# Where the weight sums stand among the blocks of an up-projection: from behind the even steps to behind the odd ones, and other side work the other way round

## The chip, the cores and the metric

The kernel runs on one core of a Trainium2 chip. A core has a matrix engine (TensorE, PE in the profile, with its weight loads as PEld), a vector engine (VectorE, DVE), a scalar engine (ScalarE, ACT), a general one (GpSimd, POOL) and a synchronising one (SyncE, SP). Each works through its own queue in order, and they wait for each other by semaphores. DMA transfers are issued from such queues too: here SP issues weight loads and residuals, POOL issues the transfers of the sums that this case is about. The metric is the device time of one execution in microseconds (us).

## The reference

The program computes two layers of an encoder on 512 tokens with 1024 channels. A layer has four branches (a convolution module and three kinds of attention), gates, an output projection, and then the part that matters here, a feed-forward network with a convolution of width 3 along the tokens:

```python
def _conv_ffn(h, w_up, conv_w, conv_b, w_down):
    u = _depthwise_conv(h @ w_up, conv_w, conv_b)
    gate, up = jnp.split(u, 2, axis=-1)
    return (jax.nn.silu(gate) * up) @ w_down

def reference(x, ...):
    for l in range(DEPTH):                    # DEPTH = 2
        h = _rmsnorm(x, g_mix[l])
        ...                                   # branches, gates
        x = x + mixed @ w_out[l]
        x = x + _conv_ffn(_rmsnorm(x, g_ffn[l]), w_up[l], ffn_conv_w[l], ffn_conv_b[l], w_down[l])
    return x
```

D_FF is 2816, so w_up is 1024 x 5632 and w_down 2816 x 1024. Everything is float32.

## The kernel before

All products run as pairs of rounded values: each operand is split into a high part and the rest (w_hi and w_lo for weights, xh and xl for activations), and each product is three matmuls, hi*hi, hi*lo, lo*hi (lines 243 to 245 of `prod`). The weights come as units of 128 x 1024 by SP (w_raw, L218); ACT writes w_hi (L222), DVE writes w_lo (L224).

**Up-projection** (`ffn`). 22 steps i; each has two blocks, the gate's (s = 0) and the up half's (s = 1), of 24 matmuls each into one of four PSUM banks (`mm`). Behind a block, DVE reads the bank with U = mm * RB (L892), which frees it, and ACT and DVE do the convolution (cy, L895 to L897), the gate (L901) and the product fl (L908). RB is the row of 1/rms of the tokens, broadcast to all partitions: `finish_norm` writes rstd to DRAM (row, L330), reads it back broadcast (raw, L334), both on POOL's queue, and ACT copies it (RB, L338). Since the matmuls run on the unnormalised input, RB is first needed by the U of the first block.

**Down-projection** (`down`). It is a Strassen-like scheme over pairs of the hidden blocks: 11 pairs j, each with a "quad" of w_down (four blocks of 128 x 512: b11, b12, b21, b22) and sums and differences of its blocks and of the activations. The activations' part, `split_pair`, is done for the first six pairs during the up-projection (`EARLY` names the steps) and for the others in `down`. The weights' part is `weight_sums(l, j)`, during the up-projection: four DVE operations (L955 to L958: t3, b12, t2, b21) on the quad in SBUF, four POOL transfers of 256 KB to DRAM (L961), and then `load_quad(l, j + 1)`, two POOL transfers of 512 KB (L948). The two buffers of a quad (`w_more`) are used again by the next quad, and in `down` by the raw weights of each third and fourth unit. So quad j+1 is loaded only when sums j are written.

`down` works through 22 units of 12 matmuls for the first two groups of products and then further units for the other three. Its first six matmuls write the mm banks (A) that the blocks of step 20 used, the next six the banks (B) of step 21's blocks, so each bank's first matmul has to wait for the U that reads it.

`turn_res(d)`, in layer 1 only, loads a tile of the residual, transposes it on DVE (L920) and writes it to DRAM in four transfers on SP (L923), since the last layer's output is token by token.

**What sets the order.** The code is written with a tile framework; a scheduler places each engine's instructions by priority, which follows the order of the code, and by when they can run in its own model. `issue_after` and `after_mm` tie the weight sums to the last matmul before them (`last_mm`), so they can't be placed ahead of it. `split_pair` and `turn_res` have no such tie. In this kernel `weight_sums(l, i // 2)` stands behind the two blocks of each even step i (0, 2, ..., 20), before the U's of that step.

## Time and profile before

| quantity | value |
|---|---|
| median of 3 runs | 1561.07 us (1560.98 to 1561.43) |
| the profiled execution, its own time | 1563.17 us |
| its span in the profile | 1561.4 us |
| PE busy | 1552.9 us, 99% of the span |
| PE clock granted | 1.00 |
| DVE busy | 1220.4 us, 78% |
| ACT busy | 833.7 us, 53% |
| POOL busy | 176.9 us, 11% |
| up-projection of layer 0, blocks | about 436 to 674 us |
| up-projection of layer 1, blocks | about 1212 to 1452 us |

Start times in the rows count from the start of the span. A row of the timeline has the start, the duration, the engine, the line, the operation, what it writes and reads, and in brackets how long its engine had been idle before it and what ended that. "SPq" and "POOL ... DMA" rows are the issue of a transfer; when the transfer lands is told by the DMA views.

### The profile page before, as it was taken

How to read it: one execution, taken by the hardware profiler on the slowest of the kernel's cores; microseconds unless marked ns; L12 is line 12 of the kernel's file. 1: busy time of each engine (PE TensorE's matmuls, PEld its weight loads, DVE VectorE, ACT ScalarE, POOL GpSimd, SP SyncE). 2: the span in 40 equal slices, each digit the busy share in tenths (PEclk: the TensorE clock that was granted, in tenths of full speed). 3: DMA queues.
4: the chain of work that ended last, by engine and by line, in shares of the span. 5: the costliest groups of instructions: out<-in, count | busy, mean ns of one | idle time of the engine just before them, and what ended most of it. 6: DMA issues, size and time to landing. Idle time of an engine off the chain costs nothing.

```text
span 1561.4 us, 20467 instructions
## 1 busy us (share of the span) xinstructions
PE 1552.9 (99%) x7198; PEld 1292.2 (83%) x7198; DVE 1220.4 (78%) x2083; ACT 833.7 (53%) x1419; POOL 176.9 (11%) x308
## 2 busy tenths in 40 slices
PE   9999999999999999999999999999999999999999
PEld 8888888888888888888888888888888788888887
DVE  6689988765679997796676899887655699987964
ACT  5678767333444443364458687772434444443643
POOL 0102002122011111100001020012120111111000
PEclk9999999999999999999999999999999999999999
DMA  7622222232646655576556422223226676665675
GB/s 231 196 93 82 84 83 82 95 100 93 213 162 209 193 190 186 200 235 212 185 183 182 120 68 86 81 72 105 95 94 222 170 228 217 213 218 194 222 226 167
DMA packets 103607, 245.41 MB, mean 157 GB/s; under 512 B 27600, under 2 KB 29520, under 8 KB 103504
## 3 DMA queue, kind: packets, MB, share of 16 engines
q1 hardware_dynamic: 89392, 196.37, 39.9%
q0 software_dynamic: 13824, 47.20, 8.9%
q8 instruction: 57, 0.93, 0.3%
q10 hardware_dynamic: 288, 0.52, 0.1%
q14 instruction: 46, 0.38, 0.1%
HBM read 203.15 MB, written 35.66 MB: 153 GB/s over the span
## 4 chain that ended last, share of the span: by engine, by line
PE 91%; DVE 4%; ACT 3%; issue 1%; DMA 1%; POOL 0%; SPq 0%; ACTq 0%; DVEq 0%; POOLq 0%
PE mm L243 21%; PE mm L244 21%; PE mm L245 21%; PE aux L1023 2%; PE aux L1024 2%; PE aux L1025 2%; PE mm L439 2%; PE mm L440 2%; PE mm L441 2%; PE mm L1024 2%; PE mm L1025 2%; PE mm L1023 2%; PE aux L709 2%; DVE w_lo L224 1%; PE aux L440 1%; PE aux L441 1%
## 5 line engine op out<-in xcount | busy, mean ns | idle before, releaser
L222 ACT ACTIVATE w_hi<-w_raw 128x1024 fp32r<-128x1024 f32 (+1 forms) x305 | 318.5, 1044 | 355.0 <-PE mm L244 193.7
L243 PE MATMUL mm<-xh,w_hi 128*128 128x512 f32 x1280 | 499.9, 391 | 1.8 <-DVE U L892 1.8
L245 PE MATMUL mm<-xh,w_lo 128*128 128x512 f32 x1280 | 498.7, 390 | 0.0
L244 PE MATMUL mm<-xl,w_hi 128*128 128x512 f32 x1280 | 498.6, 390 | 0.0
L224 DVE TENSOR_TENSOR w_lo<-w_raw,w_hi 128x1024 fp32r<-128x1024 f32 (+1 forms) x305 | 369.1, 1211 | 88.2 <-ACT w_hi L222 86.0
L243 PEld LDWEIGHTS mm<-xh,w_hi 128*128 128x128 f32 x1280 | 240.3, 188 | 51.3 <-DVE U L892 2.2
L245 PEld LDWEIGHTS mm<-xh,w_lo 128*128 128x128 f32 x1280 | 240.3, 188 | 50.4
L244 PEld LDWEIGHTS mm<-xl,w_hi 128*128 128x128 f32 x1280 | 240.4, 188 | 48.8
L813 POOL TENSOR_TENSOR mx<-mx,t 128x512 f32<-128x512 f32 x44 | 66.9, 1529 | 428.6 <-DVE t L812 327.4
L377 DVE SCALAR_TENSOR_TENSOR cv<-cv,prm 128x512 f32<-128x512 f32 x120 | 93.8, 781 | 0.7
L892 DVE TENSOR_TENSOR U<-mm,RB 128x512 f32<-128x512 f32 x88 | 60.2, 687 | 41.5 <-PE mm L245 31.3
L895 ACT ACTIVATE cy<-U,prm 128x512 f32<-128x512 f32 x88 | 70.7, 807 | 38.5 <-DVE U L892 38.4
L783 DVE TENSOR_TENSOR t<-mm,RB 128x512 f32<-128x512 f32 x64 | 44.0, 688 | 47.8 <-PE mm L245 47.4
L439 PE MATMUL mm<-w_hi,xh 128*128 128x512 f32 x192 | 76.4, 398 | 0.4 <-DVE V L567 0.4
L440 PE MATMUL mm<-w_lo,xh 128*128 128x512 f32 x192 | 75.0, 390 | 0.0
L441 PE MATMUL mm<-w_hi,xl 128*128 128x512 f32 x192 | 74.8, 390 | 0.0
L696 ACT ACTIVATE e<-e,rl 128x256 f32<-128x256 f32 (+2 forms) x96 | 57.4, 598 | 23.4 <-DVE rl L695 23.1
L897 DVE SCALAR_TENSOR_TENSOR cy<-U,prm,cy 128x512 f32<-128x512 f32 x88 | 65.7, 748 | 1.6
L901 ACT ACTIVATE fth<-cy 128x512 f32<-128x512 f32 x44 | 27.9, 633 | 71.4 <-DVE cy L897 71.3
L896 DVE SCALAR_TENSOR_TENSOR cy<-U,prm,cy 128x512 f32<-128x512 f32 x88 | 65.5, 746 | 0.4 <-ACT cy L895 0.4
L689 ACT ACTIVATE e<-e,nm 128x256 f32<-128x256 f32 (+2 forms) x96 | 57.6, 600 | 2.7
L717 DVE TENSOR_TENSOR pt<-aux,pt 128x256 fp32r<-128x256 f32 (+2 forms) x96 | 50.9, 530 | 2.4 <-ACT pt L716 1.2
(292 smaller groups left out, 2592.5 us busy)
## 6 DMA issues: line engine op xcount, KB each, us to landing
w_raw<-W SPq DMA_DIRECT2D x223, 512.0 KB, 3.6
quad<-W POOLq DMA_DIRECT2D x44, 512.0 KB, 5.2
w_raw<-W SPq DMA_DIRECT2D x66, 256.0 KB, 3.7
sums<-t POOLq DMA_DIRECT2D x44, 256.0 KB, 3.3
sums<-quad POOLq DMA_DIRECT2D x44, 256.0 KB, 3.9
w_raw<-sums SPq DMA_DIRECT2D x44, 256.0 KB, 3.9
w_raw<-sums SPq DMA_DIRECT2D x22, 512.0 KB, 4.7
res<-xn SPq DMA_DIRECT2D x24, 256.0 KB, 2.0
```

What stands on the lines that cost most here:

```text
L222: w = nc.scalar.activation(hi[:, s], raw[:, s], AF.Copy)
L224: nc.vector.tensor_tensor(lo[:, s], raw[:, s], hi[:, s].bitcast(F32), ALU.subtract)
L243: mm(ps, lhsT=wh, rhs=xh, start=start, stop=False)
L244: mm(ps, lhsT=wh, rhs=xl, start=False, stop=False)
L245: self.last_mm = mm(ps, lhsT=wl, rhs=xh, start=False, stop=stop)
L377: self.after_mm(v.scalar_tensor_tensor(acc, u[:, t:t + S], w(t), acc, ALU.mult, ALU.add))
L439: mm(pss[b], lhsT=self.Xh[k][:, t], rhs=hi[:, s], start=k == 0, stop=False)
L440: mm(pss[b], lhsT=self.Xh[k][:, t], rhs=lo[:, s], start=False, stop=False)
L441: self.last_mm = mm(pss[b], lhsT=self.Xl[k][:, t], rhs=hi[:, s], start=False, stop=k == KT - 1)
L813: (v if n == ORDER[3] and d >= 6 else nc.gpsimd).tensor_tensor(m, m, t, ALU.add)
L895: nc.scalar.activation(y, u[:, 1:513], AF.Identity, scale=w(1), bias=self.par('ffn_conv_b', c))
L897: v.scalar_tensor_tensor(y, u[:, 2:514], w(2), y, ALU.mult, ALU.add)
```

## The change

Three tables or rules move. The weight sums of pair j go behind the blocks of the odd step 2j + 1 instead of the even step 2j, but for the last pair, j = 10, which stays behind step 20. `EARLY` moves four of its six steps by one or two. `turn_res(d)` goes from the odd step 2d + 1 to the even step 2d + 2. No work is added or taken away.

```diff
-EARLY = (3, 6, 10, 13, 17, 20)
+EARLY = (4, 6, 10, 12, 16, 18)
+
+SUMS = (1, 3, 5, 7, 9, 11, 13, 15, 17, 19, 20)
 ...
-            if i % 2 == 0:
+            if i in SUMS:
 
                 with self.tc.issue_after(self.last_mm.ins):
-                    self.weight_sums(l, i // 2)
+                    self.weight_sums(l, SUMS.index(i))
 ...
-            if last and i % 2 == 1 and i // 2 < KT:
-                self.turn_res(i // 2)
+            if last and i % 2 == 0 and 0 < i // 2 <= KT:
+                self.turn_res(i // 2 - 1)
```

Below the tables every line number of the changed kernel is two higher. PE's own order is the same in both kernels. Three places show how the other engines' order moves.

**POOL, at the start of layer 1's up-projection.** row and raw are the two transfers of the broadcast, quad the load of the first quad, sums the writes of the first weight sums. Before:

```order
L948 DMA quad<-W 128x1024 x2
L330 DMA row<-rstd 128x4
L961 DMA sums_11901<-t_11895 128x512
L334 DMA raw<-row 128x512
L961 DMA sums_11901<-quad 128x512
L961 DMA sums_11901<-t_11896 128x512
```

and after the change:

```order
L950 DMA quad<-W 128x1024 x2
L332 DMA row<-rstd 128x4
L336 DMA raw<-row 128x512
L963 DMA sums_11977<-t_11971 128x512
L963 DMA sums_11977<-quad 128x512
```

The first sums' write stood between row and raw, and now stands behind both. (In layer 0 raw stood directly behind row already.)

**DVE, the last two sums of layer 0's up-projection.** U0 to U3 are the reads of the banks of successive blocks, t3 the first operation of a pair's sums. Before:

```order
L892 TENSOR_TENSOR U3_4497<-mm_6256,RB_4559 128x512
L224 TENSOR_TENSOR w_lo_6335<-w_raw_6333,w_hi_6334 128x1024
L896 SCALAR_TENSOR_TENSOR cy1_6295<-U3_4497,prm_73,cy1_6295 128x512
L897 SCALAR_TENSOR_TENSOR cy1_6295<-U3_4497,prm_73,cy1_6295 128x512
L908 TENSOR_TENSOR fl19_6299<-cy1_6295,fth_6292 128x512
L892 TENSOR_TENSOR U0_4488<-mm_6301,RB_4559 128x512
L224 TENSOR_TENSOR w_lo_6410<-w_raw_6408,w_hi_6409 128x1024
L896 SCALAR_TENSOR_TENSOR cy0_6375<-U0_4488,prm_73,cy0_6375 128x512
L897 SCALAR_TENSOR_TENSOR cy0_6375<-U0_4488,prm_73,cy0_6375 128x512
L955 TENSOR_TENSOR t3_6363<-quad_6208,quad_6207 128x512
L892 TENSOR_TENSOR U1_4491<-mm_6332,RB_4559 128x512
L224 TENSOR_TENSOR w_lo_6441<-w_raw_6439,w_hi_6440 128x1024
```

and after the change, from the end of pair 9's sums to the start of pair 10's:

```order
L958 TENSOR_TENSOR quad_6116<-quad_6116 128x512
L898 SCALAR_TENSOR_TENSOR cy1_6314<-U3_4497,prm_73,cy1_6314 128x512
L959 TENSOR_TENSOR t2_6292<-quad_6117,quad_6116 128x512
L899 SCALAR_TENSOR_TENSOR cy1_6314<-U3_4497,prm_73,cy1_6314 128x512
L960 TENSOR_TENSOR quad_6117<-quad_6117,t2_6292 128x512
L910 TENSOR_TENSOR fl19_6318<-cy1_6314,fth_6311 128x512
L894 TENSOR_TENSOR U0_4488<-mm_6320,RB_4559 128x512
L226 TENSOR_TENSOR w_lo_6410<-w_raw_6408,w_hi_6409 128x1024
L898 SCALAR_TENSOR_TENSOR cy0_6394<-U0_4488,prm_73,cy0_6394 128x512
L899 SCALAR_TENSOR_TENSOR cy0_6394<-U0_4488,prm_73,cy0_6394 128x512
L894 TENSOR_TENSOR U1_4491<-mm_6351,RB_4559 128x512
L957 TENSOR_TENSOR t3_6382<-quad_6303,quad_6302 128x512
```

Pair 10's first operation stands behind the U1 that it stood ahead of, and pair 9's sums, which stood four blocks ahead of pair 10's, now stand two ahead. Pair 9's first operation stands directly behind the two cy of block 38 and ahead of U3.

**DVE, from the last sums to the last U of layer 0.** Before:

```order
L958 TENSOR_TENSOR quad_6208<-quad_6208,t2_6364 128x512
L908 TENSOR_TENSOR fl20_6386<-cy1_6382,fth_6379 128x512
L892 TENSOR_TENSOR U2_4494<-mm_6407,RB_4559 128x512
L224 TENSOR_TENSOR w_lo_6526<-w_raw_6524,w_hi_6525 128x1024
L896 SCALAR_TENSOR_TENSOR cy0_6471<-U2_4494,prm_73,cy0_6471 128x512
L1002 TENSOR_TENSOR pfl11_6506<-fl13_5758,pxl0_6504 128x512
L897 SCALAR_TENSOR_TENSOR cy0_6471<-U2_4494,prm_73,cy0_6471 128x512
L1004 TENSOR_TENSOR sum_6511<-fl12_5682,fl13_5758 128x256
L1005 TENSOR_TENSOR fl12_5682<-fl12_5682 128x256
L1006 TENSOR_TENSOR sum_6511<-sum_6511,fl12_5682 128x256
L1010 TENSOR_TENSOR fl13_5758<-fl13_5758,sum_6511 128x256
L892 TENSOR_TENSOR U3_4497<-mm_6438,RB_4559 128x512
```

and after the change:

```order
L960 TENSOR_TENSOR quad_6303<-quad_6303,t2_6383 128x512
L910 TENSOR_TENSOR fl20_6405<-cy1_6401,fth_6398 128x512
L894 TENSOR_TENSOR U2_4494<-mm_6407,RB_4559 128x512
L226 TENSOR_TENSOR w_lo_6526<-w_raw_6524,w_hi_6525 128x1024
L1004 TENSOR_TENSOR pfl11_6506<-fl13_5777,pxl0_6504 128x512
L898 SCALAR_TENSOR_TENSOR cy0_6471<-U2_4494,prm_73,cy0_6471 128x512
L899 SCALAR_TENSOR_TENSOR cy0_6471<-U2_4494,prm_73,cy0_6471 128x512
L1006 TENSOR_TENSOR sum_6511<-fl12_5667,fl13_5777 128x256
L1007 TENSOR_TENSOR fl12_5667<-fl12_5667 128x256
L1008 TENSOR_TENSOR sum_6511<-sum_6511,fl12_5667 128x256
L894 TENSOR_TENSOR U3_4497<-mm_6438,RB_4559 128x512
L226 TENSOR_TENSOR w_lo_6544<-w_raw_6542,w_hi_6543 128x1024
```

The sequence is nearly the same: pfl11 moves ahead of both cy, and L1010 (now L1012) from ahead of the last U to behind it.

## The prediction

> **What bounds the kernel now.** I read the page from the top: the span and the busy shares, then the chain that ended last, then the groups with the idle time before them.

> ```profile
> span 1561.4 us, 20467 instructions
> PE 1552.9 (99%) x7198; PEld 1292.2 (83%) x7198; DVE 1220.4 (78%) x2083; ACT 833.7 (53%) x1419; POOL 176.9 (11%) x308
> PE 91%; DVE 4%; ACT 3%; issue 1%; DMA 1%; POOL 0%; SPq 0%; ACTq 0%; DVEq 0%; POOLq 0%
> L243 PE MATMUL mm<-xh,w_hi 128*128 128x512 f32 x1280 | 499.9, 391 | 1.8 <-DVE U L892 1.8
> ```

> PE (the matmuls) is busy in all but 1561.4 - 1552.9 = 8.5 us, and the chain runs over it for 91% of the span. The change adds and removes no matmul, so it can win no more than the PE gaps near what it moves, and it loses whatever new gap it opens. So the second view is the table of stretches over the two up-projections (columns: stretch, us, busy time of PE, PEld, DVE, ACT, POOL with counts, PE clock, DMA share, GB/s).

> ```profile
> 436.00:674.00 238.00, 238.00 (x1056) 197.23 (x1055) 203.89 (x303) 106.76 (x139) 35.71 (x66) 1.00 0.58 191
> 1212.00:1452.00 240.00, 238.20 (x1056) 197.06 (x1055) 207.39 (x311) 106.03 (x139) 35.75 (x66) 1.00 0.67 210
> ```

> Layer 0's up-projection has no PE gap, layer 1's has 240.00 - 238.20 = 1.80 us. That is all there is to win in the stages that the change touches: 2 us. DVE, with 203.89 of 238 us, is 86% busy there; it is the engine on which a misplaced wait would hurt.

> **Where the 1.80 us come from.** The timeline of layer 1's start, POOL's queue and what hangs on it, and then the same steps of layer 0:

> ```profile
> 1221.27 0.55 POOL L330 DMA_DIRECT2D row<-rstd  x1 [47.19 <-DVE rstd L275]
> 1221.92 0.55 POOL L961 DMA_DIRECT2D sums<-t  x1
> 1226.47 0.54 POOL L334 DMA_DIRECT2D raw<-row  x1 [4.00 <-DMA row<-rstd]
> 1232.75 0.39 PE L245 MATMUL mm<-xh,w_lo 128*128 128x512 f32 x1
> 1233.05 1.11 ACT L338 ACTIVATE RB<-raw 128x512 f32<-128x512 f32 x1 [9.87 <-DMA raw<-row]
> 1234.19 1.89 DVE L892 TENSOR_TENSOR U<-mm,RB 128x512 f32<-128x512 f32 x3 [8.42 <-ACT RB L338]
> 1234.94 0.50 PE L243 MATMUL mm<-xh,w_hi 128*128 128x512 f32 x1 [1.80 <-DVE U L892]
> ```
> ```profile
> 444.15 0.55 POOL L330 DMA_DIRECT2D row<-rstd  x1 [46.27 <-DVE rstd L275]
> 446.55 0.54 POOL L334 DMA_DIRECT2D raw<-row  x1 [1.85 <-DMA row<-rstd]
> 450.20 1.12 ACT L338 ACTIVATE RB<-raw 128x512 f32<-128x512 f32 x1 [3.23 <-DMA raw<-row]
> ```

> The four mm banks fill, and the fifth block cannot start until U (L892) has read the first, for which it needs RB, the broadcast of the row of rstd. In layer 0 the two POOL transfers stand next to each other: 446.55 - 444.15 = 2.40 us to the second, 450.20 - 446.55 = 3.65 more to RB. In layer 1 a 256 KB transfer of the first weight sums stands between them, and the same steps take 1226.47 - 1221.27 = 5.20 and 1233.05 - 1226.47 = 6.58. PE's matmuls start 0.23 apart, so PE was ready at 1232.75 + 0.23 = 1232.98 and started at 1234.94: 1.96 us lost, and 0.11 more in the first matmul (0.50 for 0.39), 2.07 together.

> **Part 1: the first sums leave the first step.** After the change POOL's queue in layer 1 reads row, raw, then sums, as in layer 0. By layer 0's distances RB would start at 1221.27 + 2.40 + 3.65 = 1227.32. It needs to start by 1232.98 - (1234.94 - 1233.05) = 1231.09, so 3.8 us are to spare. Bounds: the whole 2.07 is won, or nothing, where the row is late for another reason. I take -2.0, since the nearer row is layer 0's. In layer 0 nothing waits there, so nothing is won.

> What could hold the row otherwise: SP had just issued two writes of transposed residual.

> ```profile
> 1219.68 0.96 SPq L923 DMA_DIRECT2D resT<-xn  x2
> 1217.38 0.70 DVE L920 STREAM_TRANSPOSE xn<-xr 128x512 f32<-128x512 f32 x1
> 1245.07 0.69 DVE L908 TENSOR_TENSOR fl<-cy,fth 128x512 f32<-128x512 f32 x1
> 1245.80 0.42 DVE L1004 TENSOR_TENSOR sum<-fl,fl 128x256 f32<-128x256 f32 x1
> ```

> [...]

> **Part 2: EARLY and turn_res.** The last two rows show the first early pair's first instruction 0.73 us behind fl, in the second step, while the table says step 3: the scheduler takes this work when its inputs exist, not where the code stands. The same for the transposes, the first of which runs in the first block, three blocks ahead of its code. In the order of the changed kernel both stay there. Their cost is nothing, hidden in DVE's idle 32 us of these 240. If they did move, all eight transposes of 0.70 us are 5.6 us of DVE work, still inside that; each step has a share of 1.5 us.

> **Part 3: the spacing at the end.** The sums of pair j need quad j, whose load waits until the sums of pair j-1 have been written and freed its buffer. Of before, sums follow each other every two steps, 21.75 us (661.76 - 640.01 in the rows below). In the changed order they still do, but for the last: pair 9 goes behind step 19 and pair 10 behind step 20. On DVE pair 9 now starts behind the cy of 650.24, so at 650.9, and pair 10 behind the U of 663.70, so at 664.3. The gap is 13.4 us.

> ```profile
> 640.01 0.68 DVE L955 TENSOR_TENSOR t<-quad 128x512 f32<-128x512 f32 x1
> 650.40 0.54 POOL L948 DMA_DIRECT2D quad<-W  x1 [0.56 <-DMA sums<-quad]
> 1418.30 0.69 DVE L955 TENSOR_TENSOR t<-quad 128x512 f32<-128x512 f32 x1
> 1429.53 0.54 POOL L948 DMA_DIRECT2D quad<-W  x1 [1.59 <-DMA sums<-quad]
> quad<-W POOLq DMA_DIRECT2D x44, 512.0 KB, 5.2
> quad<-W POOLq DMA_DIRECT2D x2, 512.0 KB, 6.4
> DMA to landing us min/median/max: 2.6/4.8/7.1
> 650.24 0.75 DVE L897 SCALAR_TENSOR_TENSOR cy<-U,prm,cy 128x512 f32<-128x512 f32 x1
> 661.76 0.69 DVE L955 TENSOR_TENSOR t<-quad 128x512 f32<-128x512 f32 x1
> 663.70 0.69 DVE L892 TENSOR_TENSOR U<-mm,RB 128x512 f32<-128x512 f32 x1 [1.25 <-PE mm L245]
> ```

> From t of one pair to the issue of the second half of the next quad it takes 650.40 - 640.01 = 10.39 us in layer 0 and 1429.53 - 1418.30 = 11.23 in layer 1 (these are the last pairs but one, with the same neighbours on DVE). The fifth row is the page's median landing of a quad's half, 5.2; the sixth is the DMA view of 640 to 661 alone, 6.4; the seventh the shortest and longest of all transfers of that tile, 2.6 and 7.1. The turn-round is then 10.39 + 5.2 = 15.6 to 10.39 + 6.4 = 16.8 us, at the ends 13.0 to 18.3. So DVE, which takes its instructions in order, stands at t for 2.2 to 3.4 us, from nothing to 4.9 at the ends. I take 3.0, nearer to the two measured here (16.8, and 11.23 + 5.2 = 16.4).

> [...]

> What is queued behind t, and who waits:

> ```profile
> 664.61 1.23 DVE L224 TENSOR_TENSOR w_lo<-w_raw,w_hi 128x1024 fp32r<-128x1024 f32 x1 [0.22 <-ACT w_hi L222]
> 674.46 0.43 DVE L1010 TENSOR_TENSOR fl<-fl,sum 128x256 f32<-128x256 f32 x1
> 674.80 0.69 DVE L892 TENSOR_TENSOR U<-mm,RB 128x512 f32<-128x512 f32 x1
> 676.42 0.39 PE L1023 MATMUL mm<-w_hi,pe 128*128 128x512 f32 x1
> 677.36 1.22 DVE L224 TENSOR_TENSOR w_lo<-w_raw,w_hi 128x1024 fp32r<-128x1024 f32 x1 [1.27 <-ACT w_hi L222]
> 680.04 0.39 PE L1024 MATMUL mm<-w_lo,pfh 128*128 128x512 f32 x1
> 681.16 1.23 DVE L224 TENSOR_TENSOR w_lo<-w_raw,w_hi 128x1024 fp32r<-128x1024 f32 x1 [1.32 <-ACT w_hi L222]
> 696.69 0.50 PE L1024 MATMUL mm<-w_lo,pfh 128*128 128x512 f32 x1 [0.17 <-DVE w_lo L224]
> 1453.10 0.68 DVE L892 TENSOR_TENSOR U<-mm,RB 128x512 f32<-128x512 f32 x1
> 1454.71 0.39 PE L1023 MATMUL mm<-w_hi,pe 128*128 128x512 f32 x1
> ```

> From the w_lo at 664.61 DVE works without a pause: the splits of the weights of down's first two units, the rest of the sums, U of the blocks 42 and 43. Without L1010, which now stands behind U, that is 674.46 - 664.61 = 9.85 us, with t (0.6 from start to start) 10.45. Unstalled, the last U would start at 664.30 + 10.45 = 674.75, as before. Down's tenth matmul (676.42) writes the bank that this U reads; the distance from a U to its matmul was 1234.94 - 1234.19 = 0.75, so U must start by 675.67. The slack is 0.92: a stall of 3.0 delays PE by 2.1 us. In layer 1 the slack is 1454.71 - 0.75 - 1453.10 = 0.86: 2.1 again. With stalls of 2.2 to 3.5 it is 1.3 to 2.6 per layer.

> A second customer: the third and fourth weight units of down take their buffers from the quads, so their loads start when these sums are written. Their t is 5.5 us later than before (667.3 for 661.76), less the 2.2 that DVE idled between t and the w_lo at 664.61 (2.85 apart, 0.6 of it t): the sums leave about 3.3 us later. In layer 0 the third unit's w_lo ended 680.04 - 677.36 - 1.22 = 1.46 ahead of its matmul, the fourth's about 0.38 (681.16 + 1.23 = 682.39, and its matmul 2.72, twelve starts, behind 680.04). With PE itself 2.1 later the third just makes it, 1.46 + 2.1 - 3.3 = 0.3, and the fourth is short by 3.3 - 2.1 - 0.4 = 0.8. Bounds: 0, if its load meets fewer others when it starts later, and 1.0, the 0.8 and 0.2 for the wait at 696.69 (0.17), which grows from the same slack; I take 0.5, the middle. In layer 1 I add nothing: the wait for w_lo at 696.69 has no counterpart there.

> **Sum.** -2.0 (start of layer 1) + 2.1 + 0.5 (end of layer 0's up-projection) + 2.1 (layer 1's) = +2.7 us. The profiled execution took 1563.17, its span 1561.4, so 1.8 lie around it; the median of the runs is 1561.07, 2.1 lower, and the sum is put on it: 1561.07 + 2.7 = 1563.8 us.

> **The rivals.**

> A. *The quad comes in time.* For it: the shortest landing of 2.6 with 10.39 gives 13.0 < 13.4, and U has 0.9 of slack. Against it: the medians. Then only the gain is left: 1561.07 - 2.0 = 1559.1 us. Chance 0.13.

> B. *The row is not freed.* The two resT writes in the rows above, not the sums, held it. For it: they are on SP just ahead of row, in layer 1 alone. Against it: the sums' issue stands right between row and raw. Then 1561.07 + 2.1 + 2.1 + 0.5 = 1565.8. Chance 0.12.

> C. *Slower: the last quad comes later still.* The long issue time of layer 1 (11.23) and the long landing of layer 0 (6.4) meet, since the load now runs 11 us later, beside the first weights of down. It is on DVE at pair 10's t and decides from a stall of 3.5 on. For it: the two landings of 6.4. Against it: the median of 5.2 over 44 loads. The stall is 11.23 + 6.4 - 13.4 = 4.2, PE's delay 3.3 in each layer, the 0.5 as above: 1561.07 - 2.0 + 6.6 + 0.5 = 1566.2. Chance 0.15.

> D. *The change doesn't do what it says*: if the scheduler had put the sums back, the time would be 1561.1. The order of the changed kernel speaks against it. Chance 0.02.

> **The numbers.** My forecast has 0.55, and the rest of 0.03 is for a gap outside these stages that closes too. The forecast is 1563.8, its own range 1562.2 (stalls of 2.2, nothing at the fourth unit) to 1565.3 (stalls of 3.5 and the full 1.0). The range to hold the time 8 times in 10 takes in rival A, whose price is a landing inside the measured ones, and most of C: 1559.0 to 1566.5. A measurement of this kernel tells about 0.2%, 3.1 us, from no change, so 1564.2 is the bound to slower: of my own case some 0.36 lies below and 0.19 above it. Same: 0.36 + 0.13 + 0.02 = 0.51. Slower: 0.19 + 0.12 + 0.15 = 0.46. Faster: the rest, 0.03.

> **What the profile would show.** Right: in layer 1 raw's issue about 2.4 us behind row's and no PE idle behind U there; a DVE idle of 2 to 3.5 us in front of the last t, ended by the DMA quad<-W; a PE idle of 1.3 to 2.6 at the tenth matmul of down, ended by U, in both layers. Wrong: t of pair 10 without idle (A); raw again 4 us or more behind row (B); PE idle over 3 per layer (C); or pairs of sums not 13.4 us apart.

## The result

| | us |
|---|---|
| before, median of 4 runs | 1561.25 (1560.98 to 1562.31) |
| changed, median of 4 runs | 1569.70 (1569.10 to 1569.92) |
| ratio | 1.0052, 95% interval 1.0040 to 1.0064 |
| predicted | 1563.8, range 1559.0 to 1566.5 |

The change makes the kernel 8.4 us slower: a clear loss, and outside the range. The profiled execution of the changed kernel took 1569.92 us with a span of 1568.2, so like is compared with like when the two spans are: 1568.2 - 1561.4 = 6.8 us.

The page of the changed kernel has this in the rows that were shown of before:

```profile
span 1568.2 us, 20470 instructions
PE 1555.9 (99%) x7198; PEld 1292.8 (82%) x7198; DVE 1216.8 (78%) x2083; ACT 834.6 (53%) x1419; POOL 177.1 (11%) x308
quad<-W POOLq DMA_DIRECT2D x44, 512.0 KB, 5.4
```

PE is not only idle for longer (12.3 us for 8.5). It is also *busy* for 3.0 us longer with the same 7198 matmuls, for which the prediction had no term. The waits of PE and of DVE, in order of size, lead to both (the columns are the time waited, how often, and the longest):

```profile
PE mm L1025 <- DVE U L894: 5.2, 2, 2.8
PE mm L1026 <- DVE w_lo L226: 0.5, 1, 0.5
DVE t L957 <- DMA quad<-W: 7.3, 2, 3.8
```

In each layer PE waits once for U at the down-projection's first matmuls, and DVE once for the quad. The wait for U at the start of layer 1 is gone. The timeline of layer 0's end shows the chain:

```profile
651.36 0.68 DVE L957 TENSOR_TENSOR t<-quad 128x512 f32<-128x512 f32 x1
662.23 0.54 POOL L950 DMA_DIRECT2D quad<-W  x1 [0.63 <-DMA sums<-quad]
664.17 0.69 DVE L894 TENSOR_TENSOR U<-mm,RB 128x512 f32<-128x512 f32 x1 [1.82 <-PE mm L247]
668.34 0.69 DVE L957 TENSOR_TENSOR t<-quad 128x512 f32<-128x512 f32 x1 [3.48 <-DMA quad<-W]
676.67 0.39 PE L1027 MATMUL mm<-w_hi,pe 128*128 128x512 f32 x1
678.74 0.69 DVE L894 TENSOR_TENSOR U<-mm,RB 128x512 f32<-128x512 f32 x1
679.48 0.50 PE L1025 MATMUL mm<-w_hi,pe 128*128 128x512 f32 x1 [2.42 <-DVE U L894]
682.65 1.23 DVE L226 TENSOR_TENSOR w_lo<-w_raw,w_hi 128x1024 fp32r<-128x1024 f32 x1 [3.23 <-ACT w_hi L224]
683.93 0.50 PE L1026 MATMUL mm<-w_lo,pfh 128*128 128x512 f32 x1 [0.54 <-DVE w_lo L226]
```

Pair 9's t starts at 651.36; pair 10's is free to start behind U, at 664.17 + 0.60 = 664.77, and starts at 668.34. The stall is 3.57 us, the last U comes at 678.74, and PE's next matmul 0.74 later. Then the third unit's w_lo is late as well. Layer 1 has the same chain, and behind it something that layer 0 does not have (timeline, and the table of stretches with the PE clock in the third column from the right):

```profile
1444.06 0.69 DVE L894 TENSOR_TENSOR U<-mm,RB 128x512 f32<-128x512 f32 x1 [1.83 <-PE mm L247]
1448.59 0.69 DVE L957 TENSOR_TENSOR t<-quad 128x512 f32<-128x512 f32 x1 [3.84 <-DMA quad<-W]
1456.56 0.39 PE L1027 MATMUL mm<-w_hi,pe 128*128 128x512 f32 x1
1459.72 0.50 PE L1025 MATMUL mm<-w_hi,pe 128*128 128x512 f32 x1 [2.78 <-DVE U L894]
1460.66 0.63 PE L1025 MATMUL aux<-w_hi,pe 128*128 128x512 f32 x1
1461.09 0.63 PE L1026 MATMUL aux<-w_lo,pe 128*128 128x512 f32 x1
1464.15 0.39 PE L1025 MATMUL aux<-w_hi,pfh 128*128 128x512 f32 x1
```
```profile
679.40:683.40 4.00, 3.92 (x16) 2.92 (x16) 0.77 (x2) 1.84 (x3) 0.00 (x0) 1.00 0.75 280
1460.40:1463.90 3.50, 3.50 (x10) 2.75 (x9) 1.42 (x2) 2.51 (x4) 0.00 (x0) 0.52 0.68 258
```

Within 0.9 us after the idle time PE falls to half its clock: matmuls start 1461.09 - 1460.66 = 0.43 us apart instead of 0.23, for 3.4 us, and then at the full clock again. That is eight matmuls times 0.2 us, 1.6 us lost with PE busy. In layer 0, after 2.42 us of idle time, the clock stays at 1.00.

At the start of layer 1 (POOL's timeline, then the stretch of the up-projection) the order does what it should:

```profile
1225.44 0.55 POOL L332 DMA_DIRECT2D row<-rstd  x1 [47.20 <-DVE rstd L277]
1229.05 0.54 POOL L336 DMA_DIRECT2D raw<-row  x1 [3.06 <-DMA row<-rstd]
```
```profile
1212.00:1452.00 240.00, 240.00 (x1064) 198.84 (x1063) 201.36 (x303) 106.54 (x137) 34.77 (x64) 1.00 0.64 204
```

raw follows row by 3.61 us instead of 5.20, and PE has no gap in the whole up-projection.

### The profile page after: what moved, and what is told of

It reads as the page before. It is cut to its first block, busy times and chain, and to the rows that moved or that the text cites. A ratio compares the mean times of both kernels' runs of the same rounds, so it can differ in the third digit from the quotient of the medians.

```text
span 1568.2 us, 20470 instructions
## 1 busy us (share of the span) xinstructions
PE 1555.9 (99%) x7198; PEld 1292.8 (82%) x7198; DVE 1216.8 (78%) x2083; ACT 834.6 (53%) x1419; POOL 177.1 (11%) x308
## 4 chain that ended last, share of the span: by engine, by line
PE 88%; DVE 4%; ACT 3%; issue 3%; DMA 2%; POOL 0%; SPq 0%; ACTq 0%; DVEq 0%; POOLq 0%
PE mm L245 20%; PE mm L246 20%; PE mm L247 20%; PE aux L1026 3%; PE aux L1025 3%; PE aux L1027 3%; PE mm L441 2%; PE mm L443 2%; PE mm L442 2%; PE mm L1026 2%; PE mm L1027 2%; PE mm L1025 2%; PE aux L711 2%; PE aux L442 1%; PE aux L443 1%
## 5 line engine op out<-in xcount | busy, mean ns | idle before, releaser
L224 ACT ACTIVATE w_hi<-w_raw 128x1024 fp32r<-128x1024 f32 (+1 forms) x305 | 318.6, 1045 | 380.9 <-PE mm L246 216.7
L245 PE MATMUL mm<-xh,w_hi 128*128 128x512 f32 x1280 | 499.8, 390 | 0.0
L245 PEld LDWEIGHTS mm<-xh,w_hi 128*128 128x128 f32 x1280 | 240.3, 188 | 48.9
L897 ACT ACTIVATE cy<-U,prm 128x512 f32<-128x512 f32 x88 | 70.7, 806 | 25.0 <-DVE U L894 25.0
L963 POOL DMA_DIRECT2D sums<-t x44 | 24.0, 545 | 260.4 <-DVE t L957 245.3
## 6 DMA issues: line engine op xcount, KB each, us to landing
w_raw<-W SPq DMA_DIRECT2D x223, 512.0 KB, 3.5
quad<-W POOLq DMA_DIRECT2D x44, 512.0 KB, 5.4
w_raw<-sums SPq DMA_DIRECT2D x22, 512.0 KB, 5.1
```

What stands on the lines that cost most here:

```text
L224: w = nc.scalar.activation(hi[:, s], raw[:, s], AF.Copy)
L245: mm(ps, lhsT=wh, rhs=xh, start=start, stop=False)
```

## The experiments

Two things needed an answer. Is the short distance between the last two pairs the whole of the loss, or do the other edits share in it? And why is the loss on the medians (8.4 us) larger than between the two profiles (6.8)? My theory for the first: the sums of a pair cannot start before the quad's turn-round, 17 us, is over; a distance of 13.4 us makes DVE wait, and at that place nothing hides it. For the second: the gap of 2 us at layer 1's start, which the change removes, was in the profiled execution of before but not, or not so large, in the typical one.

The kernel before was run beside all of these; over its 51 runs of the three sets it took 1560.5 to 1563.5 us, with medians of 1562.02, 1561.93 and 1561.83, which is 0.6 to 0.8 above the four runs of the result. The ratios below go by the runs of the same set.

| kernel | median us | ratio to before, 95% interval |
|---|---|---|
| pair 9's sums alone late (step 19 for 18) | 1571.72 | 1.0063 (1.0050 to 1.0076) |
| only EARLY and turn_res moved | 1562.14 | 1.0001 (0.9992 to 1.0010) |
| the change, short distance in the middle | 1561.41 | 0.9996 (0.9987 to 1.0005) |
| first pair's sums alone off step 0 | 1562.79 | 1.0005 (0.9996 to 1.0014) |
| the change, last pair at step 21 | 1578.49 | 1.0111 (1.0096 to 1.0127) |
| the change, pair 9 one block earlier | 1561.12 | 0.9996 (0.9987 to 1.0005) |

### Is the gap at layer 1's start in every execution?

The kernel before, unchanged, profiled again.

> The kernel before, unchanged, profiled once more. The profiled execution took 1563.17 us, 2.1 more than the median of the other runs, and its only PE gap in the two feed-forward networks above 0.5 us was the 1.96 us behind U at the start of layer 1. Theory 'not in every run': that gap comes only when row and raw land late, so most executions do not have it; this profile shows a span of about 1559.3 us and PE without a wait at the start of layer 1. Rival 'always there': the gap is part of the kernel; the span is 1561.4 again where the time is 1563, or the gap of about 2 us stands there and the missing 2 us are elsewhere.

It took 1561.72 us, with a span of 1559.9, 1.5 below the first profile. PE's wait at that place, and POOL's two transfers:

```profile
PE mm L243 <- DVE U L892: 0.4, 1, 0.4
```
```profile
1220.89 0.55 POOL L330 DMA_DIRECT2D row<-rstd  x1 [47.19 <-DVE rstd L275]
1226.20 0.54 POOL L334 DMA_DIRECT2D raw<-row  x1 [4.11 <-DMA row<-rstd]
```

So neither theory had it quite: the gap is there, but with 0.4 us instead of 1.8. raw is as late behind row as before (5.31 us); what differs is when raw lands: RB starts at 1231.24, 5.04 us behind raw's issue instead of 6.58. Four other kernels below keep the first sums behind step 0 too, and PE's idle time at that place in their profiles is 1.2 (EARLY and turn_res alone), 0.3 (pair 9 alone), 0.9 and 0.8 us (the two with repeats of U). With the first, six executions have 0.3 to 1.8 us, 0.9 in the mean; with the slow restart of the first matmul (0.50 us for 0.39 in each) they lose 1.2 us. The first profile of before had the largest.

### Which edit costs?

Pair 9 alone moved, in the kernel before:

```diff
+SUMS = (0, 2, 4, 6, 8, 10, 12, 14, 16, 19, 20)
 ...
-            if i % 2 == 0:
+            if i in SUMS:
 ...
-                    self.weight_sums(l, i // 2)
+                    self.weight_sums(l, SUMS.index(i))
```

> The kernel before with one change: the weight sums of pair 9 stand behind step 19 instead of 18; all others, EARLY and turn_res stay. Theory 'the short last gap is all of it': DVE waits 3.5 to 4 us for the last quad in both layers, PE waits 2.4 to 3 us for the last U in both, the third and fourth unit of layer 0 wait under 1 us, and the clock is halved for 3.4 us in a layer where PE idled nearly 3 us; together about 8.5 us on the median, 1569.7 us. Rival 'the other edits share it': without the move of the first sums, EARLY and turn_res the loss is under 6 us, 1567 us or less.

And the complement, the sums where they were and the rest changed:

```diff
-EARLY = (3, 6, 10, 13, 17, 20)
+EARLY = (4, 6, 10, 12, 16, 18)
 ...
-            if last and i % 2 == 1 and i // 2 < KT:
-                self.turn_res(i // 2)
+            if last and i % 2 == 0 and 0 < i // 2 <= KT:
+                self.turn_res(i // 2 - 1)
```

> The changed kernel with the weight sums back behind the even steps: only EARLY and turn_res are moved. Theory 'the scheduler places that work by its inputs': nothing moves that PE waits for, 1561.2 us within 1 us. Rival 'the other edits share it': 1563 us or more, with a new PE wait inside the up-projections or at the start of a down-projection.

Pair 9 alone costs 9.7 us, more than the change as a whole; EARLY and turn_res together cost nothing that can be measured. The profile of the kernel with pair 9 alone (waits of DVE and PE, then stretches behind the two idle times):

```profile
DVE t L957 <- DMA quad<-W: 7.8, 2, 4.3
PE mm L1025 <- DVE U L894: 5.6, 2, 3.2
PE mm L245 <- DVE U L894: 0.3, 1, 0.3
```
```profile
679.40:683.10 3.70, 3.69 (x9) 2.96 (x10) 0.07 (x1) 1.16 (x2) 0.00 (x0) 0.54 0.80 287
1461.30:1464.90 3.60, 3.60 (x9) 2.88 (x10) 0.08 (x1) 1.17 (x2) 0.00 (x0) 0.53 0.80 287
```

The same chain as in the changed kernel, with the gap at layer 1's start kept and the clock halved in both layers. That is the expected mechanism, and the 9.7 us are 1.2 over the expected 8.5: I had counted on a halved clock where PE idles "nearly 3 us", and here 2.41 us in layer 0 were enough.

```profile
679.40 0.65 PE L1025 MATMUL mm<-w_hi,pe 128*128 128x512 f32 x1 [2.41 <-DVE U L894]
```

### Does a short distance cost anywhere, and how short is too short?

The change with its short distance elsewhere:

```diff
-SUMS = (1, 3, 5, 7, 9, 11, 13, 15, 17, 19, 20)
+SUMS = (1, 3, 5, 7, 9, 11, 12, 14, 16, 18, 20)
```

> The changed kernel with the one short distance between two pairs' sums moved from the end (steps 19 and 20) to the middle (11 and 12); behind it the sums stand on even steps as in the kernel before. Theory 'a DVE wait costs only where U has no slack': DVE may wait 2 to 4 us for a quad in the middle, PE does not, since a bank is needed again only three blocks (16 us) later; nothing at the end. The time is 1559.2 to 1561.2 us, the lower where the gap at the start of layer 1 is in all runs of before. Rival 'a short gap costs wherever it is': PE loses 2 us or more per layer in the middle, 1564 us or more.

1561.41 us, 0.2 above the expected range, span 1559.2: the whole loss is gone. DVE does stand in the middle, and PE has no wait for U or w_lo in either feed-forward network (the two t of layers 0 and 1, then POOL at layer 1's start):

```profile
580.44 0.69 DVE L957 TENSOR_TENSOR t<-quad 128x512 f32<-128x512 f32 x1 [2.75 <-issue]
1356.62 0.69 DVE L957 TENSOR_TENSOR t<-quad 128x512 f32<-128x512 f32 x1 [2.88 <-DMA quad<-W]
1221.20 0.55 POOL L332 DMA_DIRECT2D row<-rstd  x1 [47.19 <-DVE rstd L277]
1224.20 0.54 POOL L336 DMA_DIRECT2D raw<-row  x1 [2.45 <-DMA row<-rstd]
```

A wait of 2.88 us costs nothing there, where the bank that DVE is late to read is needed three blocks later. In layer 0 the profile names no releaser for the 2.75 us; the quad's second half was issued at 574.34, and with the 5.9 us that the DMA view gives for the landings there it is the same wait.

Next the smallest mend at the end itself: pair 9 one block earlier, three blocks ahead of pair 10 instead of two.

```diff
                 self.tick()
+                if i == 19 and s == 0:
+                    with self.tc.issue_after(self.last_mm.ins):
+                        self.weight_sums(l, 9)
-            if i in SUMS:
+            if i in SUMS and i != 19:
```

> The changed kernel with pair 9's sums one block earlier, behind the gate's block of step 19 instead of behind both; everything else as in the change. In the order pair 9's t then stands behind fl of step 18 (about 646.2), pair 10's t ahead of the U of block 41 again (661.8): 15.6 us apart instead of 13.4. Theory 'quad turn-round': it takes 16 to 17 us, so DVE waits 0.4 to 1.5 us at pair 10's t, most of which it idled there anyway (1.9 us until the next U); PE waits under 0.5 us at the start of down; 1560 to 1562 us. Rival 'the odd steps themselves are at fault': PE still waits 2 us or more at down's tenth matmul, 1566 us or more.

1561.12 us, span 1559.4. DVE's rows:

```profile
646.78 0.69 DVE L960 TENSOR_TENSOR t<-quad 128x512 f32<-128x512 f32 x1 [0.57 <-DMA quad<-W]
662.77 0.69 DVE L960 TENSOR_TENSOR t<-quad 128x512 f32<-128x512 f32 x1 [0.95 <-DMA quad<-W]
663.66 0.69 DVE L897 TENSOR_TENSOR U<-mm,RB 128x512 f32<-128x512 f32 x1 [0.20 <-PE mm L247]
```

The pairs are 16.0 us apart because that is how long the quad takes; DVE waits 0.95 us, in time in which it would have waited for PE anyway. Two blocks are too few and three are enough. (This kernel and the last are the fastest of the study, but neither can be told from the kernel before: both intervals hold 1.)

The other way to even the distances is to move pair 10 later:

```diff
-SUMS = (1, 3, 5, 7, 9, 11, 13, 15, 17, 19, 20)
+SUMS = (1, 3, 5, 7, 9, 11, 13, 15, 17, 19, 21)
```

> The changed kernel with the last pair's sums behind step 21 instead of 20, so that all sums stand two steps apart. Theory 'quad turn-round': DVE never waits for a quad, and the last U is not late by it. But the third unit of the down-projection takes its buffer from the last quad: before, its w_lo started 11.6 us behind L956; L956 now stands at about 675.5, so the w_lo comes at 687 for a matmul at 680: PE waits 5 to 7 us per layer, plus 1.7 where the clock is halved: 1572 to 1578 us. Rival 'even spacing is what counts': no PE wait, 1559 to 1561 us.

1578.49 us, the slowest, and 0.5 above the expected range. DVE never waits for a quad, but PE waits 6 us for the third unit of each down-projection, and the clock is halved for 6.8 us, from within the wait on: 3.3 us of it lie behind the restart in layer 0, 4.8 in layer 1 (PE's wait, and the stretches of the halved clock):

```profile
PE mm L1025 <- ACT w_hi L224: 12.2, 2, 6.2
```
```profile
682.74:689.57 6.83, 3.32 (x8) 2.53 (x9) 4.48 (x9) 2.88 (x4) 0.00 (x0) 0.50 0.72 227
1467.81:1474.63 6.82, 4.81 (x11) 3.66 (x12) 4.83 (x7) 4.41 (x6) 0.00 (x0) 0.50 0.50 172
```

So step 21 is too late for the last pair, by about 6 us.

### What held the row?

Only the first pair moved, in the kernel before:

```diff
+SUMS = (1, 2, 4, 6, 8, 10, 12, 14, 16, 18, 20)
 ...
-            if i % 2 == 0:
+            if i in SUMS:
 ...
-                    self.weight_sums(l, i // 2)
+                    self.weight_sums(l, SUMS.index(i))
```

> The kernel before with one change: the first pair's weight sums stand behind step 1 instead of 0; the short distance is then between steps 1 and 2. EARLY and turn_res stay. Theory 'the sums held the row, by a changing amount': in layer 1 raw follows row by 2.4 to 3.6 us, no PE wait at the start of layer 1, none elsewhere; span about 1559.2 us, 0.5 to 1 us less than the median of before, since before loses 0.5 to 2 us there from run to run. Rival 'the row is late by the two residual writes': raw is issued 4 us or more behind row again, PE waits 0.5 to 2 us.

Its timeline of POOL at layer 1's start and of DVE at 1289, and PE's waits:

```profile
1221.48 0.55 POOL L332 DMA_DIRECT2D row<-rstd  x1 [47.20 <-DVE rstd L277]
1224.64 0.55 POOL L336 DMA_DIRECT2D raw<-row  x1 [2.62 <-DMA row<-rstd]
1289.43 0.71 DVE L922 STREAM_TRANSPOSE xn<-xr 128x512 f32<-128x512 f32 x1 [2.12 <-DMA xr<-res]
```
```profile
PE mm L247 <- DVE w_lo L226: 0.6, 1, 0.6
PE mm L1026 <- DVE w_lo L226: 0.2, 1, 0.2
```

The first half came as expected: raw is 3.16 us behind row and PE does not wait at layer 1's start. The second did not: the span is 1560.8, the median 1562.79, no gain over before. In this order a transpose of turn_res waits 2.12 us for its residual at 1289, DVE's queue stands, a w_lo is late, and PE waits 0.6 us for it at 1294.5. By the start times of PE's matmuls, the same matmuls come 1.9 us earlier than in the first profile of before once layer 1 has started, and only 0.6 earlier from 1301 on: 1.3 of the 1.9 us are lost again there. (The 0.2 us at 697 the kernel before has too.) I had priced the start alone.

Two profiles of the kernel before with the last U repeated on DVE were to measure the clock without any change in transfers:

```diff
-                v.tensor_tensor(u[:, 1:513], ps, self.RB, ALU.mult)
+                for _ in range(1 + (i == NF - 1 and s == 1) * (5, 7)[l]):
+                    v.tensor_tensor(u[:, 1:513], ps, self.RB, ALU.mult)
```

> The kernel before with the last U of an up-projection computed again into the same tile, 5 times more in layer 0 and 7 times more in layer 1 (0.6 us each on DVE); no transfer and no other instruction changes. With a slack of 0.9 PE should idle 5 x 0.6 - 0.9 = 2.1 us in layer 0 and 3.3 in layer 1. Theory 'an idle PE loses its clock': after 3.3 us the granted clock is halved for about 3.4 us (8 matmuls at 0.427 for 0.227, 1.6 us more), after 2.1 it is not; the run is 2.1 + 3.3 + 1.7 = 7.1 us above before. Rival 'the clock in the changed kernel fell for the transfers': no halving here, since the transfers are those of before: 5.4 us above.

> As the last kernel, with 7 repeats in layer 0 and 5 in layer 1: PE should idle 3.3 us in layer 0 and 2.1 in layer 1. Theory 'an idle PE loses its clock': now layer 0 has the halved clock for 3.4 us; layer 1 has it only if a shorter idle time is enough at another phase. Rival 'it belongs to layer 1': the halved clock comes in layer 1 again, or nowhere.

Both missed their aim (one execution each, 1567.36 and 1566.69 us). The scheduler spread the repeats over the next 10 us and put PE's second product with that bank later, so PE waited for weights, not for U, and never longer than 1.2 us at a time. Their mean granted clocks were 1.000 and 0.999, and they tell nothing of an idle time of 2 us or more.

### How often does the clock fall?

The changed kernel twice more, for a profile.

> The changed kernel, unchanged, profiled once more. Theory 'an idle PE of 2.4 us or more can lose its clock, by where it falls in time': PE idles 2.3 to 2.6 us in layer 0 and 2.8 to 3.2 in layer 1 again; the clock is halved for 3.4 us in layer 1, in layer 0 in some executions (the kernel with pair 9 alone late had it there after 2.41). Rival 'the halved clock of the profile was an accident': none this time, with the same idle times and a span 1.7 us shorter.

> The same once more, for the same question: does the halved clock come with the idle time each time, in which layer, and how much longer is the span with two of them than with one (by the rule of 8 matmuls 0.2 us longer each: 1.6 to 1.7 us).

Spans of 1568.2 and 1567.3 us. The stretches behind the two idle times, of the one and of the other:

```profile
679.40:683.40 4.00, 3.64 (x16) 2.63 (x14) 0.96 (x1) 2.06 (x3) 0.00 (x0) 1.00 0.74 273
1460.50:1463.90 3.40, 3.40 (x10) 2.66 (x9) 1.30 (x2) 2.39 (x4) 0.00 (x0) 0.56 0.67 257
```
```profile
679.40:683.40 4.00, 4.00 (x19) 3.13 (x18) 1.86 (x3) 2.81 (x4) 0.00 (x0) 1.00 0.67 248
1460.50:1463.90 3.40, 3.40 (x10) 2.63 (x9) 3.09 (x4) 2.87 (x5) 0.00 (x0) 0.55 0.65 233
```

In all three profiles of the changed kernel the clock is halved in layer 1 and not in layer 0. The length of the idle time alone does not decide it, since 2.41 us halved the clock in layer 0 of the kernel with pair 9 alone, and 2.42 to 2.54 us did not in layer 0 of the changed kernel, three times.

What does order them is where in time the idle time falls. The slow stretches, cut to where the clock is 0.50 throughout, last 3.41 us, or 6.83 in the kernel with the last pair at step 21. Where a profile has one in each layer, 778.24 us lie between the end of the first (683.01, and 689.57) and the start of the second (1461.25, and 1467.81), which is 228 times 3.4133. So in these two profiles the changes of the clock fit a grid of 3.413 us. Taken for all five profiles, which is an estimate, steps of that length back from a slow stretch give the windows in which the idle times lie. For the first profile of the changed kernel these are, in layer 0 and in layer 1, the window in which the idle time begins and the next:

```profile
675.25:678.67 3.42, 1.81 (x8) 1.15 (x7) 3.35 (x7) 1.78 (x4) 0.00 (x0) 1.00 0.76 173
678.67:682.08 3.41, 2.60 (x11) 2.17 (x12) 0.75 (x2) 0.52 (x1) 0.00 (x0) 1.00 0.71 228
1456.91:1460.32 3.41, 0.63 (x4) 0.52 (x4) 2.68 (x6) 0.63 (x1) 0.00 (x0) 1.00 0.89 248
1460.32:1463.73 3.41, 3.41 (x10) 2.67 (x9) 1.25 (x2) 2.34 (x4) 0.00 (x0) 0.50 0.71 270
```

In layer 0 an edge cuts the 2.42 us into 3.42 - 1.81 = 1.61 and 3.41 - 2.60 = 0.81; in layer 1 the 2.78 us lie within one window, and the next is slow. All ten idle times above 2 us, cut in this way:

| profile | layer 0: PE idle per window, us | slow windows behind | layer 1: PE idle per window, us | slow windows behind |
|---|---|---|---|---|
| the changed kernel, first | 1.61, 0.81 | none | 2.78 | 1 |
| second | 1.85, 0.66 | none | 2.96 | 1 |
| third | 1.94, 0.61 | none | 0.80, 2.15 | 1 |
| pair 9 alone late | 2.41 | 1 | 3.23 | 1 |
| last pair at step 21 | 2.71, 3.41, 0.09 | 2 | 0.51, 3.41, 2.01 | 2 |

A window with 1.94 us of idle PE or less left the clock full, and one with 2.15 us or more was followed by a slow one (so was the 2.01 us in a window that was slow already). The transfers do not order the cases: in layer 0 the DMA engines were busy for 0.73 of the window that cost the clock in the kernel with pair 9 alone, and for 0.76, 0.68 and 0.64 of the three that didn't in the changed kernel. No run shifted an idle time against the grid on purpose, so this orders the ten cases and is not tested beyond them. The comparison of one slow stretch with two in the same kernel did not come about, since none of the three profiles had two.

## Why the prediction was wrong

**The place and the chain were right.** The two t are 664.77 - 651.36 = 13.4 us apart as worked out from the order, DVE stalls at the second in both layers, the last U is late by the stall less a slack, PE stands at the tenth matmul of down, and in layer 0 the third unit's weights come late on top. The slack was put at 0.92 and 0.86; it was 3.57 - 2.58 = 0.99 (PE's loss of 2.58 from 676.67 + 0.23 to 679.48). EARLY and turn_res cost nothing, as said. Of the signs named ahead, DVE's idle time of 3.48 us and PE's of 2.42 in layer 0 lie inside the bounds, layer 1's 3.84 and 2.78 above them; raw came 3.61 us behind row, not 2.4, which was early enough.

**What failed** is the price of the stall: the sum put PE's loss at the length of its idle time, with nothing for the clock, and the stall itself, its second customer and the gain at the start were mis-sized. Term by term:

| term | predicted us | measured us |
|---|---|---|
| stall at pair 10's t, layer 0 and 1 | 3.0, 3.0 | 3.57, 3.93 |
| PE's delay by U, layer 0 (with the slow first matmul) | 2.1 | 2.7 |
| the same, layer 1 | 2.1 | 3.0 |
| third and fourth units, layer 0, net | 0.5 | 1.0 |
| halved clock, layer 1 | none | 1.6 |
| start of layer 1, on a typical execution | -2.0 | -1.2 |
| sum | +2.7 | about +7.1 |

PE's delay in layer 1 is 1459.72 - 1456.56 - 0.23 = 2.93 us and 0.11 in the slow first matmul. The third unit costs 683.93 - 683.01 - 0.23 = 0.69 (683.01 is the start of the matmul before) and 0.11 again. By the start times of PE's matmuls against those of before, the fourth costs 0.4, and the 0.2 that before lost at 696.69 is gone. Some 1.3 of the 8.4 us on the medians are in none of these terms. Part of it is the first set: in the third set the changed kernel's two executions lay 8.1 and 7.3 us above the median of before.

One sum of the prediction does not come out either: the lower end of its own range, with stalls of 2.2 and nothing at the fourth unit, is 1561.07 - 2.0 + 1.3 + 1.3 = 1561.7, not 1562.2.

1. *The clock, which the sum left out.* This is the largest single miss, and the one that no bound covered. The prediction priced an idle PE at the length of the idle time. The profile of before has no PE idle time as long in its matmul stages, so there was no row for it; the nearest was the 1.80 us at 1234.94, after which the first matmul alone is slower (0.50 us for 0.39). In the first profile of the changed kernel the clock stood at 0.50 for 3.41 us behind the 2.78 us of idle time in layer 1. By the table of windows 2.15 us of idle time within one were enough and 1.94 were not, so a delay of 2.1 us, about 1.9 of it idle, might have been safe: so this miss hangs on the third, the stalls that were longer than priced.

2. *The gain of 2.0 was taken from one execution and put on the median of others.* The profiled execution of before took 2.1 us more than that median, and I wrote both numbers down one behind the other without asking what the 2.1 us were. They were this gap for the most part: it varies from 0.3 to 1.8 us of idle time over six profiles, the first profile had the largest, and the second, 1.45 us shorter, lost 1.4 us less at this place. The median run had less left to win; the correction of 0.8 us in the table is the average over the six. It also explains 0.9 of the 1.6 us between 8.4 us (medians) and 6.8 us (spans), since the first profile lost 2.1 there and the average is 1.2. Against the profile of before itself the measured terms give 2.7 + 1.0 + 3.0 + 1.6 - 2.1 = 6.2 us of the 6.8; 0.5 of the rest lies in the first 6 us of the program, ahead of all that the change touches.

3. *The turn-round.* I put it at 16.4 us; from pair 9's t to pair 10's it took 668.34 - 651.36 = 17.0 in layer 0, and with the stall of 3.93 on the same distance 17.3 in layer 1. Rival C's long issue time came about half way (10.87 us to the issue at 662.23, between 10.39 and 11.23) and its long landing nearly (6.1 more to t), and with them a stall just beyond the 3.5 from which C was to decide. C's chain was right, though PE idled 2.42 and 2.78 us and not the over 3 of its sign; its price of 1566.2 was too low, since it lacked the clock and took the whole 2.0 at the start of layer 1. The page's median landing of 5.2, which spoke against C, was too short for these two loads; why they took longer is not shown.

Rival A's case, a quad in time, failed by 3.6 and 3.9 us. The shortest landing of 2.6 that spoke for it stands against 5.4 us in the median of a quad's half here and about 6 at this place. Rival B was wrong: with the residual writes still ahead of it, raw came 3.00 us behind row (the short distance in the middle), 3.16 (first pair alone), 3.64 (pair 9 one block earlier) and 3.22 to 3.61 (the changed kernel, three profiles) with the first sums moved, and 5.20 and 5.31 (before, two profiles), 5.17 (EARLY and turn_res alone), 5.03 and 5.57 (the two with repeats of U) with them in their place. It was the first sums that held the row's completion, which came 4.9 us after its issue in the profile of before and 3.3 in the first of the changed kernel; of their transfers only one write, issued 0.65 us *behind* the row on the same queue, stood between row and raw. What is left between 3.0 and layer 0's 2.40 may be the residual writes; that was not tried.

**The chances.** 0.46 for slower and a range to 1566.5 rested on the stall only. With the clock as a condition of its own, "each PE idle time of over 2 us in a matmul stage costs 1.6 more or nothing", the upper end would have been 1569.7, where the median fell.

## What to carry to other kernels

Before a step of a pipeline through reused buffers is moved, work out the turn-round of its buffer (compute, store, free, load) and compare it with the new distance at every place; a short distance is free where what it delays has slack (the middle here) and costs nearly in full (all but 1 us of the stall here) at a border where the next stage needs the same engine and the same buffers. Price a new idle time of the matrix engine not at its length alone but with the slow clock that can follow: here seven of the ten idle times above 2 us were followed by 3.41 us or more at half the clock, which cost 1.6 us in the changed kernel. And before a gap in one profiled execution is counted as a gain, compare that execution's own time with the median: if it is slower by about the gap, take a second profile first.
